# A planner inside the kernel that sets the order in which every engine is queued (hybrid encoder step, one core)

## The chip, the core and the metric

The kernel runs on one core of a Trainium2 chip. Its engines are named as the profile names them: PE is the matrix engine (PEld its weight loads), DVE the vector engine, ACT the scalar engine, POOL the GpSimd engine, SP the engine that issues the DMAs. Each engine works through one queue in order. The metric is the device time of one execution in microseconds (us); lower is better.

## The reference, cut to what matters

One layer of a streaming encoder is computed for 2048 prompt frames and 32 sample frames of width 1024, which share the weights. Every sub-layer is wrapped in an RMSNorm before and one after:

```
h  = rmsnorm(x);  qa,ka,va,qb,kb,vb,g_low,r = split(h @ w_in)
oa = band_attention(qa, ka, va)         # 8 heads x 64, own 64-frame chunk and the 8 before, relative bias
ob = gla_recurrence(qb, kb, vb, gates)  # 4 heads, key 64, value 128
x  = x + rmsnorm(concat(oa, norm(ob) * silu(r)) @ w_o)
mk, mv = rmsnorm(mem) @ w_mk, rmsnorm(mem) @ w_mv
x  = x + rmsnorm(softmax((h @ w_mq) mk^T) mv @ w_mo)           # 4 heads x 256, 256 memory tokens
x  = x + rmsnorm((silu(h @ w_gate) * (h @ w_up)) @ w_down)     # hidden width 2816
```

All arithmetic is in float32; the new keys, values, states and memory keys and values are outputs too.

## The kernel before

The 2080 frames are handled in three stages, which this document calls A, B and C. Between them only DRAM buffers are passed on (names ending in d: x1d, h1d, h2d, x2d), and each stage opens SBUF and PSUM pools of its own.

- Stage A is the parallel mixing: projections (tiles wqa, wka, wva, wvr), band attention (scores s, softmax u, its transposes pt, prt, products po, o), the linear attention (names that begin with g), the memory keys and values (mkps, mkf, mkt; mvps, mvf), and the output projection w_o (wops), whose rows of 512 or 544 frames are normalised and scaled at lines 751 and 759 (tiles y, acc). The projection of the first memory queries (mqps0) is in it too.
- Stage B is the memory attention in five blocks of 416 frames: queries mqps, scores ms, transposes mpt, values mpv, output mops. A block ends in mem_fin: norm n3, residual (L1000, L1001), norm n4, scaling (L1005). Squares are summed by DVE and POOL (L104), and a matmul with ones (n3_4, n4_4 for the last block) spreads the sum.
- Stage C is the SwiGLU in three blocks of two halves, each product of four blocks done as seven: X, Y and Z are its PSUM tiles (pg for gate, pu for up), mf0 to mf6 the seven operands of a block, made by ffn_ops from the rows hr; pdn is the down projection, which DVE adds into acc.

A float32 product is done as three float32r matmuls: split() writes a rounded copy on ACT (L84) and subtracts it from the source on DVE or POOL (L88), for weights (wg_s, wu_s, wd, wmo_s, wo_s from raw tiles ending in _r) and activations (mf, mv, om) alike:

```
def split(hi, lo, src, lo_eng=None):
    ACT.copy(hi, src)
    ...
    lo_eng.tensor_tensor(out=lo, in0=src, in1=hi.bitcast(F32), op=ALU.subtract)
```

The kernel's Python traces the instructions in program order. Work of two kinds is interleaved as it is traced: weave() sorts lists of work items by their relative place, so that attention and projections alternate. The order in which an engine's queue is filled is then set by the framework's scheduler, which follows the data, the buffers and a priority. The priority is the program order, pulled forward by hand in places: high_priority(offset=PRI) with PRI = 4000 for weight loads and their splits, 8000 for the last mem_fin, and led() with offsets of -3000 to 3000 for single operations. The scheduler works over the stage seams: weights of stage C are loaded and split while stage B still runs.

Of the kernel before, what the change touches and what calls it, by code (L numbers as in the profile page):

```python
# [2 lines left out]

# [5 lines left out]
F32 = mybir.dt.float32  # L9
F32R = mybir.dt.float32r  # L10
# [3 lines left out]
PSUM = bass.MemoryType.PSUM  # L14
DRAM = bass.MemoryType.DRAM

P = 128
# [24 lines left out]
    return out  # L42


@with_exitstack
def encoder_step(ctx, tc, ins, outs):
    nc = tc.nc
    PE, ACT, DVE, POOL, SP = nc.tensor, nc.scalar, nc.vector, nc.gpsimd, nc.sync
# [6 lines left out]
    dpool = ctx.enter_context(tc.tile_pool(name="dpool", bufs=1, space=DRAM))  # L55
    RW = dict(reuse_waits="tile")

    PRI = 4000
    QLEAD = 0.5
    ident = cpool.tile([P, P], F32, name="ident")  # L60
    with tc.high_priority(offset=2 * PRI):
        SP.dma_start(ident, ins["c_ident"])
# [33 lines left out]
    def norm_fm(pool, pspool, xs, n, name, tag="dense", rbufs=2):  # L96
        acc = pool.tile([P, n], F32, tag="nacc", name=name + "_acc")
        for k in range(KT):
            if k == 0:
                ACT.activation(acc, xs[k], AF.Square)  # L100
            else:
                sq = pool.tile([P, n], F32, tag="nsq", name=f"{name}_sq{k}")
                ACT.activation(sq, xs[k], AF.Square)
                (POOL if k % 2 else DVE).tensor_tensor(out=acc, in0=acc, in1=sq, op=ALU.add)  # L104
        ps = pspool.tile([P, 512], F32, tag=tag, name=name + "_ps")
        PE.matmul(ps[:, :n], lhsT=ones, rhs=acc, start=True, stop=True)
        return rstd_of(pool, ps[:, :n], n, D, name + "_r", rbufs)
# [8 lines left out]
    def w_piece(wp, src, name, lo_eng=None):  # L116

        kk, m = src.shape[1], src.shape[2]
        with tc.high_priority(offset=PRI):
            raw = wp.tile([P, 544], F32, tag="wraw", name=name + "_r")[:, : kk * m].rearrange("p (k m) -> p k m", k=kk)  # L120
# [24 lines left out]
    def weave(*lists, lead=1.0):  # L145

        todo = [((i + 0.5) / len(items) * (1.0 if li else lead), li, i, it) for li, items in enumerate(lists) for i, it in enumerate(items)]
        return [it for *_, it in sorted(todo, key=lambda x: x[:3])]
# [36 lines left out]
    with ExitStack() as ph:  # L185
# [13 lines left out]
        def xtile(name):  # L199
            return xp.tile([P, 1088], F32, tag="xw", name=name)  # L200


        def norm_tile(src, tn, g, x_dst, h_dst, name, t_in=None, t_out=None, dst=None):

            xt = xtile(name + "_xt")[:, :D] if t_in is None else t_in
            with tc.high_priority(offset=0 if t_in is None else 2 * PRI):
                SP.dma_start(xt[:tn], src)
# [161 lines left out]
        anti = up.tile([P, P], F32, tag="prt", bufs=2, name="anti")  # L369
# [56 lines left out]
        turn = [0]  # L426
# [274 lines left out]
        def merge(*lists, lead=1.0):  # L701
            for it in weave(*lists, lead=lead):
                it()
# [102 lines left out]
        def mem_q0():  # L806
            n = CB[0][1]
            mv = {}

            def first():  # L810
                mv.update(load_mov(h1d[0][:, :n], n, "hq0"))

            def query(m):
                w = load_w(wp, ins["w_mq"][0], m * P, P, f"wmq0_{m}")
                ps = pd.tile([P, 512], F32, tag="dense", name=f"mqps0_{m}")
                mm3(ps[:, :n], [(w[k], (mv[k][:, 0, :n], mv[k][:, 1, :n])) for k in range(KT)])
                qf = sp.tile([P, 544], F32, tag="st", name=f"qf0_{m}")[:, :n]
                ACT.mul(qf, ps[:, :n], 0.0625)
                SP.dma_start(qmd[0][m * P : (m + 1) * P, :], qf)

            return [first] + [partial(query, m) for m in range(KT)]
# [12 lines left out]
        for b in range(NB):  # L834
# [8 lines left out]
            elif b == NB - 2:  # L843
                kv1, kv2 = mem_kv()
                o1, o2, fin = out_proj(0)
                dense = proj(b + 1, mvs[b + 1])
                dense = dense[:-2] + o1 + dense[-2:] + o2 + kv1[:1] + weave(fin, kv1[1:])
            else:
                p1, p2, pfin = out_proj(1)
                o1, o2, fin = out_proj(2)  # L850
                q0 = mem_q0()
                dense = p1 + p2 + kv2[:1] + weave(pfin, kv2[1:]) + o1 + o2 + q0[:1] + weave(fin, q0[1:])
            merge(attn(b), dense, lead=LEAD[b])
        o1, o2, fin = out_proj(NB - 1)
        merge(o1 + o2 + fin)


    lo_set[0] = [POOL, DVE]
    dense_lead[0] = 0
    with ExitStack() as ph:  # L860
# [28 lines left out]
        def mem_h(b):  # L889
            s, n = CB[b]  # L890
            mv = []
            for k in range(KT):
                raw = hp.tile([P, 416], F32, tag="hr", name=f"h1_{b}_{k}")
                for bb, lo, hi, off in pieces(BLK, s, s + n):
                    led(200, SP.dma_start, raw[:, off : off + hi - lo], h1d[bb][k * P : (k + 1) * P, lo:hi])
                m_ = (mpa if k < 5 else mpb).tile([P, 2, 416], F32R, tag="mov", name=f"m2_{b}_{k}")
                split(m_[:, 0], m_[:, 1], raw)
                mv.append(m_)
            return mv
# [77 lines left out]
        def mem_out(b, mo):  # L977
            s, n = CB[b]
            y = []

            def tile_m(m):
                w = load_w(wp, ins["w_mo"][0], m * P, P, f"wmo{b}_{m}")
                ps = pd.tile([P, 512], F32, tag="dense", name=f"mops{b}_{m}")
                mm3(ps[:, :n], [(w[k], (mo[k][:, 0], mo[k][:, 1])) for k in range(KT)])
                yt = xps[b % 2].tile([P, 416], F32, tag="xy", name=f"y2_{b}_{m}")
                led(3000, DVE.tensor_copy, yt, ps[:, :n])
                y.append(yt)

            return [partial(tile_m, m) for m in range(KT)] + [partial(mem_fin, b, y)]

        def mem_fin(b, y):
            s, n = CB[b]
            last = b == len(CB) - 1
            with tc.high_priority(offset=2 * PRI if last else 0):
                r = norm_fm(np_, pn, y, n, f"n3_{b}")
# [14 lines left out]
        out = []  # L1010
        for b in range(len(CB)):
            mo, heads = mem_attn(b)
            fill = [partial(mem_q, b + 1, mv, m) for m in range(KT)] if b + 1 < len(CB) else out
            for it in weave(heads, fill, lead=QLEAD):
                it()
            if b + 2 < len(CB):
                mv = mem_h(b + 2)
            out = mem_out(b, mo)
            if b != len(CB) - 2:
                for it in out:  # L1020
                    it()


    wph.close()
# [3 lines left out]
    with ExitStack() as ph:  # L1028
# [60 lines left out]
        def unit_w(src, g, name):  # L1089

            with tc.high_priority(offset=PRI):
                raw = []
# [52 lines left out]
        for b, (s, n) in enumerate(CF):  # L1145
# [16 lines left out]
            def down_w(f):  # L1162

                row = []
                with tc.high_priority(offset=PRI):
                    raw_d = wp.tile([P, KT, P], F32, tag="wraw", name=f"wd{b}_{f}_r", bufs=WRB)
# [112 lines left out]
            last = b == len(CF) - 1  # L1279
            held = None  # L1280
            for g in range(NF // 2):
# [6 lines left out]
                if g and not (last and g == NF // 2 - 1):  # L1288
                    down([g - 1], [held])
                    held = None  # L1290
                if g < NF // 2 - 1 or not last:
                    held = u
# [4 lines left out]
            else:  # L1297
# [7 lines left out]
                down(gs, us, (0,), dn)  # L1305
                finish_rows(0, xts)


_INS = ["x_prompt", "x_sample", "mem_prompt", "cache_a_k", "cache_a_v", "state_gla", "cache_mem_k", "cache_mem_v",
        "g_pre_mix", "w_in", "w_alpha2", "b_alpha", "g_gla_out", "w_o", "g_post_mix", "g_pre_mem", "g_mem",  # L1310
# [48 lines left out]
```

## Time and profile before

| | |
|---|---|
| median of 3 runs | 3494.17 us (3490.74 to 3494.37) |
| the profiled execution | 3494.23 us, of which the span is 3492.5 us |
| PE busy | 3314.3 us, 95% of the span, 22211 matmul records |
| DVE, ACT, POOL busy | 2346.2, 1677.8, 1328.7 us |
| mean granted clock of PE | 0.975 |
| DMA | 488.56 MB, 140 GB/s |

A matmul of plain float32 has two records, so 22211 records stand for 20341 matmuls. The span runs from the first to the last instruction. An idle time in the profile is put down to the operation that ended it.

### The profile page before, as it was taken

How to read it: one execution, taken by the hardware profiler on the slowest of the kernel's cores; microseconds unless marked ns; L12 is line 12 of the kernel's file. 1: busy time of each engine (PE TensorE's matmuls, PEld its weight loads, DVE VectorE, ACT ScalarE, POOL GpSimd, SP SyncE). 2: the span in 40 equal slices, each digit the busy share in tenths (PEclk: the TensorE clock that was granted, in tenths of full speed). 3: DMA queues.
4: the chain of work that ended last, by engine and by line, in shares of the span. 5: the costliest groups of instructions: out<-in, count | busy, mean ns of one | idle time of the engine just before them, and what ended most of it. 6: DMA issues, size and time to landing. Idle time of an engine off the chain costs nothing. (4 is left out here: it accounts for less than half of the span.)

```text
span 3492.5 us, 60178 instructions
## 1 busy us (share of the span) xinstructions
PE 3314.3 (95%) x22211; PEld 3115.0 (89%) x22211; DVE 2346.2 (67%) x4395; ACT 1677.8 (48%) x3733; POOL 1328.7 (38%) x1086
## 2 busy tenths in 40 slices
PE   8999999999998989899999789999899999999998
PEld 6888888989987778789999689999899999899998
DVE  5578767665558687486666685666976667866665
ACT  5455455554445555465555443333543334533334
POOL 3242132132134433444543453333453334533332
PEclk9999999999999999999999899999999999999999
DMA  9855644555347455664645542222242223222222
GB/s 274 273 179 161 206 147 152 163 172 159 121 134 227 142 182 174 206 213 146 192 150 169 174 133 78 78 73 73 87 144 73 75 78 94 91 92 73 73 73 90
DMA packets 550044, 488.56 MB, mean 140 GB/s; under 512 B 48488, under 2 KB 496801, under 8 KB 549749
## 3 DMA queue, kind: packets, MB, share of 16 engines
q1 hardware_dynamic: 549749, 484.71, 45.0%
q8 instruction: 174, 2.85, 0.3%
q14 instruction: 121, 0.99, 0.1%
HBM read 369.68 MB, written 114.91 MB: 139 GB/s over the span
## 5 line engine op out<-in xcount | busy, mean ns | idle before, releaser
L81 PE MATMUL pdn<-u,wd 128*128 128x346 f32 (+1 forms) x3168 | 528.0, 324 | 11.5 <-DVE up L1049 9.8
L81 PEld LDWEIGHTS pdn<-u,wd 128*128 128x128 f32 x3168 | 511.8, 191 | 14.0 <-DVE up L1049 10.4
L84 ACT CAST wg_s<-wg_r 128x512 fp32r<-128x512 f32 x231 | 139.5, 620 | 409.5 <-PE pdn L81 200.4
L81 PE MATMUL pg_X<-mf,wg_s 128*128 128x346 f32 (+1 forms) x1584 | 283.9, 328 | 8.7 <-DVE mf L88 3.3
L1049 DVE TENSOR_TENSOR acc<-acc,pdn 128x346 f32<-128x346 f32 (+1 forms) x464 | 231.0, 510 | 87.1 <-PE pdn L81 87.0
L81 PE MATMUL pu_X<-mf,wu_s 128*128 128x346 f32 (+1 forms) x1584 | 282.2, 323 | 0.0
L81 PEld LDWEIGHTS pg_X<-mf,wg_s 128*128 128x128 f32 x1584 | 260.8, 193 | 12.6 <-ACT mf L84 4.6
L81 PEld LDWEIGHTS pu_X<-mf,wu_s 128*128 128x128 f32 x1584 | 258.1, 190 | 0.4
L88 POOL TENSOR_TENSOR wu_s<-wu_r,wu_s 128x512 fp32r<-128x512 f32 x132 | 175.8, 1333 | 212.1 <-ACT wu_s L84 202.9
L88 POOL TENSOR_TENSOR wg_s<-wg_r,wg_s 128x512 fp32r<-128x512 f32 x99 | 136.3, 1378 | 299.6 <-ACT wg_s L84 289.0
L81 PE MATMUL wvr_ps<-wvr_s,mv 128*128 128x256 f32 (+3 forms) x1632 | 222.8, 286 | 1.3 <-DVE wvr_s L88 1.3
L81 PE MATMUL wops<-om,wo_s 128*128 128x512 f32 (+1 forms) x960 | 203.8, 363 | 15.4 <-ACT om L84 14.5
L81 PE MATMUL mops<-mo,wmo_s 128*128 128x416 f32 x960 | 201.8, 360 | 12.1 <-DVE wmo_s L88 8.7
L88 POOL TENSOR_TENSOR u<-sg,u 128x346 fp32r<-128x346 f32 (+1 forms) x132 | 134.9, 1033 | 195.9 <-ACT u L84 195.9
L81 PEld LDWEIGHTS wvr_ps<-wvr_s,mv 128*128 128x128 f32 (+1 forms) x1632 | 202.9, 183 | 6.0 <-DVE wvr_s L88 1.8
L81 PEld LDWEIGHTS mops<-mo,wmo_s 128*128 128x128 f32 x960 | 179.7, 192 | 18.2 <-DVE wmo_s L88 9.5
L81 PEld LDWEIGHTS wops<-om,wo_s 128*128 128x128 f32 x960 | 157.0, 194 | 39.9 <-ACT om L84 15.3
L448 PE MATMUL po<-prt,v 128*128 128x128 f32 x1120 | 177.0, 282 | 12.0 <-DVE o L453 6.5
L84 ACT CAST wu_s<-wu_r 128x512 fp32r<-128x512 f32 x231 | 136.4, 618 | 87.5 <-DVE wu_r L1049 34.1
L448 PEld LDWEIGHTS po<-prt,v 128*128 128x128 f32 x1120 | 153.7, 195 | 19.6 <-DVE o L453 7.7
L81 PE MATMUL mqps<-m,wmq_s 128*128 128x416 f32 x768 | 163.0, 361 | 6.1 <-DVE wmq_s L88 6.1
L81 PEld LDWEIGHTS mqps<-m,wmq_s 128*128 128x128 f32 x768 | 143.0, 191 | 9.9 <-DVE wmq_s L88 7.0
(410 smaller groups left out, 7884.3 us busy)
## 6 DMA issues: line engine op xcount, KB each, us to landing
wg_r<-in_w_ffn_gate_dram SPq DMA_DIRECT2D x66, 512.0 KB, 3.8
wu_r<-in_w_ffn_up_dram SPq DMA_DIRECT2D x66, 512.0 KB, 4.2
wd_r<-in_w_ffn_down_dram SPq DMA_DIRECT2D x66, 512.0 KB, 3.5
wmq_r<-in_w_mq_dram SPq DMA_DIRECT2D x80, 256.0 KB, 2.9
wmo_r<-in_w_mo_dram SPq DMA_DIRECT2D x80, 256.0 KB, 2.9
wo_r<-in_w_o_dram SPq DMA_DIRECT2D x64, 256.0 KB, 3.1
ks<-kad SPq DMA_DIRECT2D x28, 512.0 KB, 5.1
wvr_r<-in_w_in_dram SPq DMA_DIRECT2D x48, 256.0 KB, 3.3
```

What stands on the lines that cost most here:

```text
L81: return f(*a, **k)
L84: ACT.copy(hi, src)
L88: lo_eng.tensor_tensor(out=lo, in0=src, in1=hi.bitcast(F32), op=ALU.subtract)
L448: PE.matmul(po[:, e * P : e * P + n], lhsT=v[:kk, j, :], rhs=prt[:kk, j, :n], start=j == 0, stop=j == len(rows) - 1)
L1049: eng.tensor_tensor(out=out, in0=a, in1=b, op=ALU.add)
```

## The change

A class Order is added. At the end of each stage order.queue() is called; it takes the instructions traced since the last call, and adds an edge without a semaphore from each instruction to the next one on the same engine, in the order that it has planned. The instructions, the tiles and the pools stay as they are, and so do weave, the priorities and the leads, which from here on decide only where no edge does (between stages, and among instructions that the planner leaves out, such as table loads).

The plan is made by laying the stage out in time. Each instruction has a duration and a delay until others see its result (_cost). _read works out who waits for whom from the cells of the tiles that are read and written. _pass then runs the stage forward: an engine that is free takes the ready instruction with the best rank, provided that the pool buffers it needs are free; SP's DMAs take 450 ns to issue and land after a bandwidth model. The first ranks are the framework's priorities. Afterwards the stage is run backward, and the distance of each instruction to the end of that run becomes its rank; after three such rounds the shortest plan is kept. Nothing is known of other stages: each plan starts with idle engines and ends with its own last instruction.

```
+class Order:
+    ENGINES = ("PE", "Activation", "DVE", "Pool", "SP")
+    SLOW = 1.1
+    PASSES = 3
...
+    def _cost(self, ins, kind, eng, outs, inps):
+        n = self._free(outs[0])
+        slow = self.SLOW
+        if eng == "PE":
+            if any(a.tensor.name.startswith(("ident", "anti")) for a in inps):
+                return (max(30.0, n * 0.86) if n < 128 else 110.0), 250.0
...
+            t = n * 0.4385 + 6.5
+            return (max(t, 111.0 if n >= 128 else 60.0) if n < 256 else t), 250.0
+        if eng == "SP":
+            return 450.0, 2200.0
...
+        elif eng == "Activation":
+            if kind == "InstActivation":
+                t = 170 + n * 0.9 + (195 if len(outs) > 1 else 0)
+            else:
+                t = 165 + n * (0.87 if outs[0].dtype == F32R else 0.82)
+        elif eng == "Pool":
+            t = 170 + n * 2.35
+        elif kind == "InstTensorCopy":
+            t = 150 + n * 1.05
+        elif kind == "InstTensorTensor":
+            t = 200 + n * 1.15
...
+        elif kind == "InstTensorScalarPtr":
+            t = 120 + n * 0.83 if len(inps) < 3 else (230 + n * 1.75 if n > 256 else 200 + n * 1.4)
...
+        return t * slow, 90.0
...
+    def _pass(self, prio, back=None):
...
+                for e, heap in enumerate(ready):
+                    while idle[e] and heap:
+                        _, i = heappop(heap)
+                        stop = None
+                        for k in self.uses[i]:
+                            g = self.tag[k]
+                            if not held[k] and (free[g] <= 0 or head[g] != place[k] or (back is None and self.first[k] != i)):
+                                stop = g
+                                break
...
+                        start[i] = now
+                        fin = now + dur[i]
...
+                            if e == 4:
+                                moved = max(moved, fin) + self.size[i] / 300.0
+                                seen = max(fin + 1900.0, moved + 1300.0)
...
+    def queue(self):
...
+        for turn in range(self.PASSES + 1):
+            start, end = self._pass(prio)
+            if best is None or max(end) < best[0]:
+                best = (max(end), start)
+            if turn == self.PASSES:
+                break
+            back, fin = self._pass([-(s + d) for s, d in zip(start, self.dur)], back=end)
+            whole = max(fin)
+            prio = [whole - b for b in fin]
+        start = best[1]
+        tail = {}
+        for i in sorted(range(n), key=lambda i: (start[i], i)):
+            e = self.eng[i]
+            if e in tail:
+                self.tc.add_manual_dep(self.ops[i], self.ops[tail[e]].name, self.edge, reason="order of issue")
+            tail[e] = i
...
+    order = Order(tc)
...
+    order.queue()
```

Line numbers in the new kernel are 302 higher from the body of encoder_step on. The pieces below are the order of the built programs, before and after, at three places. A name ends in the number of its tile; "x8" stands for eight equal instructions in a row.

The first place is DVE's queue in stage A, where block 0's output rows y1_0 are scaled (L759, after: L1061) while the keys of the memory are projected; mkf5 is the copy of such a projection out of PSUM, which PE then transposes. Before:

```order
L571 TENSOR_SCALAR g12_la_13144<-g12_z_13142 128x256
L572 SCALAR_TENSOR_TENSOR g12_la_13144<-g12_la_13144,g12_z_13142 128x256
L88 TENSOR_TENSOR om1_7_13176<-om1_r7_13174,om1_7_13176 128x512
L759 SCALAR_TENSOR_TENSOR y1_0_0_11344<-y1_0_0_11344,g_pre_mem_1172,acc1_0_11348 128x512 x2
L759 SCALAR_TENSOR_TENSOR y1_0_1_11345<-y1_0_1_11345,g_pre_mem_1172,acc1_0_11348 128x512 x2
L759 SCALAR_TENSOR_TENSOR y1_0_2_11346<-y1_0_2_11346,g_pre_mem_1172,acc1_0_11348 128x512 x2
L759 SCALAR_TENSOR_TENSOR y1_0_3_11347<-y1_0_3_11347,g_pre_mem_1172,acc1_0_11348 128x512 x2
L575 TENSOR_TENSOR g12_la_13144<-g12_la_13144 128x256
L785 COPY mkf5_13007<-mkps5_12982 128x256
```

The eight scalings stand in one run ahead of mkf5. The same part of DVE's queue after:

```order
L390 TENSOR_TENSOR wmk6_4_s_13031<-wmk6_4_r_13029,wmk6_4_s_13031 128x512
L1061 SCALAR_TENSOR_TENSOR y1_0_0_11344<-y1_0_0_11344,g_pre_mem_1172,acc1_0_11348 128x512
L1087 COPY mkf5_13007<-mkps5_12982 128x256
L1061 SCALAR_TENSOR_TENSOR y1_0_0_11344<-y1_0_0_11344,g_pre_mem_1172,acc1_0_11348 128x512
L1061 SCALAR_TENSOR_TENSOR y1_0_1_11345<-y1_0_1_11345,g_pre_mem_1172,acc1_0_11348 128x512 x2
L1061 SCALAR_TENSOR_TENSOR y1_0_2_11346<-y1_0_2_11346,g_pre_mem_1172,acc1_0_11348 128x512
L877 TENSOR_TENSOR g12_la_13144<-g12_la_13144 128x256
L1087 COPY mkf6_13059<-mkps6_13034 128x256
```

One scaling is left ahead of mkf5; the rest stands behind it and between other work.

The second place is PE's queue at the seam from stage B to stage C. Before:

```order
L81 MATMUL mops4_7_23159<-mo4_3_1_22619,wmo4_7_4_s_23156 128x416 x3
L106 MATMUL n3_4_ps_23209<-n3_4_acc_23186,ones_66 128x416
L81 MATMUL pg0_0_X_23437<-mf0_0_23374,wg0_0_s0_23412 128x348 x12
L81 MATMUL pg0_0_Y_23438<-mf0_1_23378,wg0_0_s1_23417 128x348
L81 MATMUL pg0_0_Z_23439<-mf0_5_23392,wg0_0_s5_23431 128x348
L81 MATMUL pu0_0_X_23566<-mf0_0_23374,wu0_0_s0_23541 128x348 x12
```

In between stand 128 matmuls of stage C before n4_4 comes. After:

```order
L383 MATMUL mops4_7_23159<-mo4_3_1_22619,wmo4_7_4_s_23156 128x416 x3
L408 MATMUL n4_3_ps_22869<-n4_3_acc_22846,ones_66 128x416
L408 MATMUL n3_4_ps_23209<-n3_4_acc_23186,ones_66 128x416
L408 MATMUL n4_4_ps_23277<-n4_4_acc_23254,ones_66 128x416
L383 MATMUL pg0_0_X_23437<-mf0_0_23374,wg0_0_s0_23412 128x348 x12
L383 MATMUL pg0_0_Y_23438<-mf0_1_23378,wg0_0_s1_23417 128x348 x12
```

n4_3 and n4_4 have moved ahead of the first matmul of C. On DVE the scalings of blocks 3 and 4 of stage B stand ahead of most of C's first subtractions now, and on ACT the splits of C's first weights but one stand behind B's last squares.

The third place is DVE's queue at the seam between blocks 0 and 1 of stage C, where the operands mf1 of block 1 are made from hr1 while pu0_10 and pdn0_9 run. Before:

```order
L1046 TENSOR_TENSOR hr1_01_26887<-hr1_11_26890,hr1_01_26887 128x4x346
L88 TENSOR_TENSOR mf1_1_27738<-hr1_00_26884,mf1_1_27738 128x4x346
L88 TENSOR_TENSOR wd0_20_0_27905<-wd0_20_r_27903,wd0_20_0_27905 128x512
L1049 TENSOR_TENSOR up0_10_01_27463<-pu0_10_c2_27629,pu0_10_Y_27625 128x348
L1046 TENSOR_TENSOR hr1_00_26884<-hr1_11_26890,hr1_00_26884 128x4x346
L1049 TENSOR_TENSOR acc0_1_23400<-acc0_1_23400,pdn0_9_0_1_27775 128x348
L1049 TENSOR_TENSOR acc0_1_23400<-acc0_1_23400,pdn0_9_1_1_27783 128x348
```

Large subtractions stand ahead of the first copy to up, and alternate with the additions to acc. After:

```order
L1463 TENSOR_TENSOR sg0_10_10_27462<-sg0_10_10_27462,pu0_10_X_27624 128x348
L1352 TENSOR_TENSOR hr1_01_26887<-hr1_11_26890,hr1_01_26887 128x4x346
L390 TENSOR_TENSOR wd0_21_0_27913<-wd0_21_r_27911,wd0_21_0_27913 128x512
L390 TENSOR_TENSOR mf1_1_27738<-hr1_00_26884,mf1_1_27738 128x4x346
L1352 TENSOR_TENSOR hr1_00_26884<-hr1_11_26890,hr1_00_26884 128x4x346
L390 TENSOR_TENSOR mf1_4_27749<-hr1_01_26887,mf1_4_27749 128x4x346
L390 TENSOR_TENSOR mf1_2_27743<-hr1_00_26884,mf1_2_27743 128x4x346
L1352 TENSOR_TENSOR hr1_10_26893<-hr1_10_26893,hr1_00_26884 128x4x346
L1355 TENSOR_TENSOR acc0_1_23400<-acc0_1_23400,pdn0_9_0_1_27775 128x348
```

The copies to up and the products sg have moved ahead of the large subtractions, and the additions to acc behind them.

More of the change, by code (lines that the diff above doesn't have):

```diff
@@ L2 @@
 from functools import partial
+from heapq import heappop, heappush
 import concourse.bass as bass
@@ L1021, in encoder_step @@
                     it()
+    order.queue()
     wph.close()
@@ L1306, in encoder_step @@
                 finish_rows(0, xts)
+    order.queue()
 _INS = ["x_prompt", "x_sample", "mem_prompt", "cache_a_k", "cache_a_v", "state_gla", "cache_mem_k", "cache_mem_v",
```

220 lines of the change are left out of this document (added).

## The prediction

> **What bounds the kernel now.** The first view is the busy time of each engine by stretch, cut at the stage seams that the timeline shows. Its columns are the stretch, its length, the busy time of each engine with the count of its instructions, the granted TensorE clock, the DMA share and GB/s.
>
> ```profile
> core 0: us, PE busy (x) PEld busy (x) DVE busy (x) ACT busy (x) POOL busy (x), PEclk, DMA share, GB/s
> 0.00:30.00 30.00, 16.70 (x96) 15.05 (x96) 16.33 (x39) 17.87 (x45) 14.48 (x36) 0.83 0.85 220
> 30.00:1480.00 1450.00, 1372.25 (x10455) 1217.52 (x10456) 967.54 (x2216) 753.33 (x1840) 471.49 (x409) 0.97 0.59 180
> 1480.00:1935.00 455.00, 438.40 (x2529) 418.79 (x2527) 309.40 (x535) 255.81 (x605) 198.29 (x142) 0.99 0.55 172
> 1935.00:2040.00 105.00, 73.07 (x332) 64.45 (x333) 84.47 (x87) 46.26 (x81) 57.86 (x38) 0.80 0.58 180
> 2040.00:2450.00 410.00, 408.75 (x2560) 406.88 (x2560) 260.72 (x426) 169.04 (x330) 160.73 (x130) 1.00 0.26 82
> 2450.00:2560.00 110.00, 97.57 (x573) 92.99 (x572) 100.60 (x127) 54.99 (x96) 61.00 (x43) 0.94 0.28 89
> 2560.00:2940.00 380.00, 379.92 (x2396) 379.32 (x2395) 238.10 (x393) 151.73 (x298) 146.27 (x121) 1.00 0.28 89
> 2940.00:3050.00 110.00, 97.29 (x570) 92.01 (x569) 100.54 (x129) 55.04 (x98) 61.50 (x43) 0.94 0.28 87
> 3050.00:3440.00 390.00, 390.00 (x2463) 389.93 (x2464) 237.87 (x398) 154.58 (x304) 149.57 (x124) 1.00 0.28 85
> 3440.00:3492.50 52.50, 40.33 (x251) 38.09 (x250) 30.63 (x53) 19.18 (x42) 7.50 (x7) 0.89 0.23 69
> sum 3492.50, PE 3314.27 PEld 3115.05 DVE 2346.18 ACT 1677.83 POOL 1328.70; mean PE 331.43 PEld 311.50 DVE 234.62 ACT 167.78 POOL 132.87
> ```
>
> PE is the bound everywhere: 3314.3 of 3492.5 us. An order of the same instructions can take two things from it: its idle time, 178.2 us, and the clock. The clock is low only in stretches that hold waits: 1.00 where PE is idle for 1.25 us or less (2040 to 2450, 2560 to 2940, 3050 to 3440), 0.80 where it is idle for 31.9 of 105 us. Stage A (30 to 1480) has 77.8 us of idle time, stage B (1480 to 1935) 16.6, the seam from B to C (1935 to 2040) 31.9, the two seams between blocks of C 12.4 and 12.7, head and tail 13.3 and 12.2. The steady parts of C, 1180 us, have nothing to give.
>
> One wait shows how the clock follows it (the third row is the longest wait of stage A):
>
> ```profile
> 219.51 0.33 PE L81 MATMUL s<-ks,qs 128*128 128x128 f32 x1 [2.18 <-DVE u_mn L81]
> 221.00:228.00 7.00, 7.00 (x25) 5.00 (x26) 6.25 (x8) 2.24 (x6) 3.71 (x3) 0.53 0.55 168
> 1443.01 0.82 PE L81 MATMUL wops<-om,wo_s 128*128 128x272 f32 x2 [10.71 <-ACT om L84]
> ```
>
> After 2.18 us of waiting the clock stands at 0.53 for 7 us, a loss of about 3.3 us. For a stretch the loss is at most its length times one minus the clock; since some of that time is itself idle, I count four fifths: 1450 x 0.03 x 0.8 = 35 us in stage A, 455 x 0.01 x 0.8 = 3.6 us in B. The Trainium skill ("TensorE: Matmul & The Clock Gate", section "HAM oscillation — how this bites in real kernels") sets the limit higher, no idle gaps of more than about 3.4 us; the trace differs with its 2.18 us. By that rule only three waits of stage A (10.7 us, and 4.9 and 4.0 in the list below) would cost clock, the clock term would be near 10 us, and the time below would come out at about 3426 us.
>
> **What PE waits for in stage A.** The waits of PE from 30 to 1430 us: engine, line, the waited-for engine and line, then us, times and the longest.
>
> ```profile
> PE s L81 <- DVE u_mn L81: 7.1, 6, 2.6
> PE po L448 <- DVE o L453: 6.5, 5, 2.6
> PE po L448 <- ACT prt L499: 5.2, 5, 1.7
> PE mkt L789 <- DVE mkf L785: 5.1, 2, 4.9
> PE mvps L81 <- DVE mvf L800: 4.0, 1, 4.0
> PE wops L81 <- ACT om L84: 3.8, 3, 2.5
> PE pt L498 <- ACT prt L499: 3.7, 6, 1.3
> PE g_o L639 <- DVE at L628: 3.4, 5, 1.6
> PE g_s L624 <- DVE g_W L604: 2.9, 1, 2.9
> PE wqa_ps L81 <- ACT mv L84: 2.6, 2, 2.1
> PE ss L81 <- DVE sks L278: 2.4, 1, 2.4
> ```
>
> They add up to 46.7 us, of which DVE's are 31.4 (67%), and with the casts of om and mv on ACT 37.8 (81%). These are short operations that stood late in a queue. The longest shows it:
>
> ```profile
> 1093.00 9.44 DVE L759 SCALAR_TENSOR_TENSOR y<-y,g_pre_mem,acc 128x512 f32<-128x512 f32 x8 [0.17 <-ACT acc L734]
> 1103.16 0.69 PE L789 MATMUL mkt<-ident,mkf 128*128 128x128 f32 x2 [4.93 <-DVE mkf L785]
> ```
>
> Eight scalings that nobody hurries for hold DVE for 9.44 us, and the copy of mkf, for which PE waits 4.93 us, stands behind them. In the new order the copy of mkf5 stands behind one scaling, and the others are spread: the planner ranks by the longest path to the stage's end, and PE's path goes through the copy.
>
> **The change, term by term.** Nothing is added or removed: the same 20341 matmuls, 1882 DMAs and vector work, every queue rewritten, SP's and POOL's too. So each term is a wait that goes, stays or is made.
>
> *Stage A.* At stake are 77.8 + 35 = 112.8 us. Waits of the kind shown should go, 67% to 81% by the list; I take three quarters, 84.6 us. The ends are one third (38 us: the planner's figures miss the chip's, and the waits turn up elsewhere) and all of it (113 us).
>
> *Stage B.* 16.6 + 3.6 = 20.2 us by the same three quarters: 15.2 us, ends 5 and 20.
>
> *The seam from B to C.* Each call plans its own stage, and in the new PE order every matmul of C stands behind n4_4, the last of B; before, 128 of them stood ahead of it. The groups of 1935 to 2040 us give the prices (last column: idle time before, and its releasers):
>
> ```profile
> L81 PE MATMUL mops<-mo,wmo_s 128*128 128x416 f32 x168 | 39.2, 390 | 10.7 <-DVE wmo_s L88 7.8 <-DVE y L81 1.6 <-ACT mo L971 1.2
> L106 PE MATMUL n_ps<-n_acc,ones 128*128 128x416 f32 x4 | 2.6, 746 | 2.8 <-POOL n_acc L104 2.8
> L1000 DVE SCALAR_TENSOR_TENSOR y<-y,g_post_mem,n_r 128x416 f32<-128x416 f32 x15 | 18.2, 1279 | 0.0
> L1001 DVE TENSOR_TENSOR y<-y,xr 128x416 f32<-128x416 f32 x4 | 4.3, 1068 | 0.0
> L104 DVE TENSOR_TENSOR n_acc<-n_acc,n_sq 128x416 f32<-128x416 f32 x9 | 7.0, 780 | 2.8 <-POOL n_acc L104 1.5 <-ACT n_sq L103 1.2
> L1005 DVE SCALAR_TENSOR_TENSOR y<-y,g_pre_ffn,n_r 128x416 f32<-128x416 f32 x8 | 7.6, 1004 | 0.0
> L1046 DVE TENSOR_TENSOR hr<-hr,hr 128x1392 f32<-128x1392 f32 x4 | 11.3, 2821 | 0.0
> L88 DVE TENSOR_TENSOR mf<-hr,mf 128x1392 fp32r<-128x1392 f32 x5 | 9.1, 1814 | 5.0 <-ACT mf L84 5.0
> ```
>
> What goes: the 10.7 us of mops, which waited behind C's weights on DVE. What comes: between n3_4 and n4_4 DVE has eight L1000 (10.2 us), four L1001 (4.3), three L104 (2.3) and eight scalings L1005 of block 3 (8.0, of which about 2.3 lie under ACT's Ln and Exp), 22.5 us, and about 2 us of POOL's last addition and the matmul: 24.5 us in which PE has nothing. Behind it twelve matmuls run (3.6 us at half clock), while DVE owes eight L1005 (8.0), two L1046 (5.6), one L88 (1.8) and a short weight operation (0.7) to the second operand: 12.5 us more. With the 2.8 us before n3 and 5 us of small waits that is 45 against 31.9 us: 13 us lost. With POOL out of the way these DVE operations could take half of their means here (end: 2 us gained); with more contention it is 55 us (23 lost).
>
> *The seams inside C.* PE waits where DVE's preparation of the next block stands ahead of the copies out of PSUM:
>
> ```profile
> 2464.62 7.01 PE L81 MATMUL pdn<-u,wd 128*128 128x348 f32 x24 [4.91 <-DVE up L1049]
> L1046 DVE TENSOR_TENSOR hr<-hr,hr 128x1384 f32<-128x1384 f32 x4 | 8.4, 2109 | 0.0
> L88 DVE TENSOR_TENSOR wd<-wd_r,wd 128x512 fp32r<-128x512 f32 x3 | 8.0, 2654 | 0.0
> L88 DVE TENSOR_TENSOR mf<-hr,mf 128x1384 fp32r<-128x1384 f32 x4 | 7.8, 1961 | 0.0
> ```
>
> In the new order the copies into up come first, and then six large subtractions and one wd stand in a row ahead of the additions to acc: 6 x 2.04 + 2.65 = 14.9 us. PE can fill six PSUM buffers of six matmuls meanwhile, 36 x 0.159 (379.92 us for 2396) = 5.7 us. So it waits about 9 us in place of 4.9; the rest of the seam (7.5 us of 12.4) should about halve, because the long scalings of the first output, which held DVE as 6 and 2, now stand as 3, 1 and 4 with weight operations between them. Gain and loss cancel: 0, ends 18 us gained and 17 lost for both seams.
>
> *Head and tail.* Chains of one thing after another, 13.3 and 12.2 us idle: 0, ends 5 either way.
>
> **The sum** against the profiled execution's 3494.2 us (span 3492.5 and 1.7 around it; the median of the runs is 3494.17): 3494.2 - 84.6 - 15.2 + 13 = 3407 us.
>
> **The rivals.**
> *Nearly every wait goes.* For it: the planner multiplies its durations off PE by 1.1, so it plans a copy rather too late than too early, and PE has work behind it. Nine tenths of A and B (120 us), no loss at B to C, 9 us at C's seams: 3365 us.
> *The waits only move.* For it: DVE is busy for two thirds of stage A, and a queue in a fixed order passes each delay on. A third of A and B (45), 13 lost at the seam and 5 in C: 3467 us.
> *Slower.* The mechanism is DVE's unbroken runs at the three seams, held up by POOL. The planner prices a 512-wide subtraction at (200 + 512 x 1.15) x 1.1 = 868 ns whatever POOL does; the wd row shows 2654. At the far ends the seams cost 23 + 17 us and 5 us of clock. It decides once A and B give less than 38 us; at a quarter of theirs (33) and a few lost at the head it ends at 3508 us. The Trainium skill ("SBUF — State Buffer", section "Who interferes with whom") speaks for it: a VectorE instruction with two SBUF inputs and a GpSimd instruction that reads SBUF share a port pair, and the later one is blocked for the whole instruction. The wd row agrees in kind; by that rule alone the seams cost the 40 us above, and the sum would be about 3434 us.
> *No change that can be measured* (0.2%, 7 us): gains and losses cancel by chance. That the order isn't changed at all is out: hardly a row of PE's queue stands where it stood.
>
> **Chances.** Forecast 0.50 (own range 3385 to 3440, from half to all of A and the ends of the seams), nearly everything 0.20, moved waits 0.17, slower 0.08, no change 0.05. Faster by over 0.2% thus 0.87, same 0.05, slower 0.08. The range 3355 to 3472 takes in the forecast, most of the first rival and most of the second.
>
> **What would show it.** Stage A with some 25 us of PE idle time in place of 78 and a clock of 0.99; no wait of mkt for mkf above 1 us; PE idle for over 20 us between the last mops and the first pg_X, and no mops wait for wmo_s; at the seams of C a wait of pdn for acc of 4 to 14 us; busy sums of ACT and POOL within a few per cent. The prediction is wrong if stage A keeps more than half of its idle time, or if B to C costs under 30 or over 55 us.

## The result, and the profile after

The changed kernel takes 3461.35 us (median of four runs, 3458.72 to 3463.02); the kernel before, run beside it on the same chip, 3493.72 us. The ratio is 0.9908 (95% interval 0.9891 to 0.9925). The kernel is 32 us faster, and the forecast was 87 us.

The head of the page of the changed kernel: PE, DVE and POOL have as many instructions as before, and the busy sums are close to those of before (DVE 2% more).

```profile
span 3456.9 us, 60285 instructions
PE 3282.8 (95%) x22211; PEld 3095.9 (90%) x22211; DVE 2395.7 (69%) x4395; ACT 1692.9 (49%) x3730; POOL 1352.5 (39%) x1086
```

PE's idle time is 3456.9 - 3282.8 = 174.1 us, where it was 178.2: the sum hides a gain and a loss of nearly the same size. To find them, both traces are cut where PE has done the same share of its matmul work (each matmul counted with the time from its start to the next one's where nothing holds PE), so that a row of one kernel is as much work as the row of the other. One cut is the prediction's seam between A and B, 1480 us, which in the changed kernel is 1411 us. The columns are the stretch, its length, PE's busy time, the granted clock, the DMA share and GB/s. Before:

```profile
340.00:1035.00 695.00, 680.66 (x5581) 0.99 0.52 158
1035.00:1480.00 445.00, 390.55 (x2746) 0.95 0.60 185
1480.00:1593.00 113.00, 105.06 (x643) 0.97 0.57 179
1593.00:1912.00 319.00, 310.34 (x1753) 0.99 0.57 174
1912.00:2063.00 151.00, 118.74 (x605) 0.86 0.53 166
2425.00:2560.00 135.00, 122.57 (x730) 0.95 0.27 87
```

The same work after the change:

```profile
334.00:1000.00 666.00, 665.20 (x5597) 1.00 0.56 168
1000.00:1411.00 411.00, 385.46 (x2750) 0.96 0.62 188
1411.00:1546.00 135.00, 109.55 (x609) 0.86 0.65 196
1546.00:1861.00 315.00, 309.84 (x1801) 0.99 0.57 173
1861.00:2016.00 155.00, 112.62 (x586) 0.81 0.51 162
2376.00:2518.50 142.50, 122.30 (x735) 0.93 0.28 84
```

Row by row: the first half of stage A became 29 us shorter, its second half 34, the seam from A to B 22 us longer, the rest of stage B 4 shorter, the seam from B to C 4 longer, the first seam in C 7.5 longer. Of the rows not shown, the second seam in C is 7 us longer, the start of A 6 us shorter, the steady parts of C and the tail together 3. That is the whole 35.6 us between the two spans. Inside stage A the planner did most of what was forecast. At the seams, where a planned stage begins or one of C's blocks gives way to the next, nothing was gained, and some 40 us of the 69 were given back.

The two longest waits of PE at the seam from A to B (1425 to 1480 us):

```profile
PE mpv L383 <- ACT vTp L386: 14.5, 1, 14.5
PE mqps L383 <- DVE m L390: 5.2, 1, 5.2
```

The first is followed back from ACT to SP. The cast of vTp had waited 12.6 us for a DMA, and that DMA was issued behind the last results of stage A (the releaser of a row stands in brackets; SPq is the DMA queue's own engine):

```profile
1473.47 0.62 ACT L386 CAST vTp<-vr 128x512 fp32r<-128x512 f32 x1 [12.61 <-DMA vr<-mvd]
```

```profile
1461.76 5.19 SPq L1062 DMA_DIRECT2D h1d<-y  x8
1468.27 0.32 SPq L383 DMA_DIRECT2D xr<-x1d  x1
...
1469.11 0.51 SPq L1190 DMA_DIRECT2D vr<-mvd  x1
```

SP's order shows why. In the kernel before, vr0, the first load of the memory's values, stood well ahead of these results. In the plan of stage B it stands behind xr0_0, a load for the end of B's block 0. Between the two planned chains the framework decides by priority, and xr0_0, traced late, has a low one: every DMA of A's last block goes first, and all that stands behind xr0_0 in B's chain waits with it.

```
1196 L383 DMA h1_2_0_18510<-h1d1_163 128x192
1197 L423 DMA wmq1_3_4_r_18325<-in_w_mq_dram 128x4x128
1198 L383 DMA h1_2_0_18510<-h1d2_164 128x224
1199 L1052 DMA x0r3_2_17591<-x0d3_73 128x544
1200 L1055 DMA x1d3_161<-y1_3_0_17047 128x544
...
1215 L1062 DMA h1d3_165<-y1_3_3_17050 128x544 x2
1216 L383 DMA xr0_0_18882<-x1d0_158 128x416
1217 L423 DMA wmq1_4_0_r_18358<-in_w_mq_dram 128x4x128
1218 L1190 DMA vr0_17734<-mvd_168 128x2x256
```

At the seam from B to C the forecast wait is there, 27.0 us between n3_4 and n4_4:

```profile
PE n_ps L408 <- POOL n_acc L406: 29.0, 2, 27.0
```

In stage C PE waits for the additions to acc, as forecast, but longer. DVE's queue and PE's at the first seam of C:

```profile
2407.49 3.10 DVE L1463 TENSOR_TENSOR sg<-sg,up 128x348 f32<-128x348 f32 x1
2410.52 0.50 DVE L1355 TENSOR_TENSOR up<-pu_c,pu_Z 128x348 f32<-128x348 f32 x1
2410.94 4.25 DVE L1463 TENSOR_TENSOR sg<-sg,up 128x348 f32<-128x348 f32 x2
...
2415.54 1.59 DVE L1352 TENSOR_TENSOR hr<-hr,hr 128x1384 f32<-128x1384 f32 x1
...
2428.06 1.36 DVE L1355 TENSOR_TENSOR acc<-acc,pdn 128x348 f32<-128x348 f32 x3
```

```profile
2409.77 4.93 PE L383 MATMUL pdn<-u,wd 128*128 128x348 f32 x30
2415.67 1.22 PE L383 MATMUL pdn<-u,wd 128*128 128x348 f32 x6 [0.97 <-DVE sg L1463]
2428.62 3.81 PE L383 MATMUL pdn<-u,wd 128*128 128x348 f32 x12 [11.73 <-DVE acc L1355]
```

The six subtractions and the wd take 12.5 us in a row (2415.54 to 2428.06). PE had filled five of its six PSUM buffers (30 matmuls) before that row began, and stopped 1.2 us into it.

### The profile page after: what moved, and what is told of

The parts are those of the page before. It is cut to its first block, busy times and chain, and to the rows that moved or that the text cites. A ratio compares the mean times of both kernels' runs of the same rounds, so it can differ in the third digit from the quotient of the medians.

```text
span 3456.9 us, 60285 instructions
## 1 busy us (share of the span) xinstructions
PE 3282.8 (95%) x22211; PEld 3095.9 (90%) x22211; DVE 2395.7 (69%) x4395; ACT 1692.9 (49%) x3730; POOL 1352.5 (39%) x1086
## 4 chain that ended last, share of the span: by engine, by line
PE 49%; DVE 4%; issue 2%; ACT 1%; DMA 1%; POOL 1%; SPq 0%; DVEq 0%; POOLq 0%; ACTq 0%
PE pdn L383 14%; PE pg_X L383 7%; PE pu_X L383 7%; PE mops L383 5%; PE pg_Y L383 3%; PE pu_Y L383 3%; PE mqps L383 2%; PE pg_Z L383 2%; PE pu_Z L383 2%; PE mpv L383 1%; PE ms L383 1%; DVE y L1304 1%; DVE hr L1352 0%; DVE acc L1535 0%; DVE mf L390 0%
## 5 line engine op out<-in xcount | busy, mean ns | idle before, releaser
L383 PE MATMUL pdn<-u,wd 128*128 128x346 f32 (+1 forms) x3168 | 521.9, 323 | 27.8 <-DVE acc L1355 25.5
L390 POOL TENSOR_TENSOR wu_s<-wu_r,wu_s 128x512 fp32r<-128x512 f32 x132 | 192.1, 1465 | 250.9 <-ACT wu_s L386 245.1
L383 PE MATMUL mops<-mo,wmo_s 128*128 128x416 f32 x960 | 191.1, 354 | 0.0
L383 PEld LDWEIGHTS mops<-mo,wmo_s 128*128 128x128 f32 x960 | 178.2, 188 | 3.7 <-issue 1.1
L750 PE MATMUL po<-prt,v 128*128 128x128 f32 x1120 | 169.6, 278 | 0.0
L383 PE MATMUL pg_Y<-mf,wg_s 128*128 128x346 f32 (+1 forms) x792 | 142.2, 328 | 14.4 <-ACT mf L386 8.3
```

Source lines behind the costliest of these rows:

```text
L383: return f(*a, **k)
L750: PE.matmul(po[:, e * P : e * P + n], lhsT=v[:kk, j, :], rhs=prt[:kk, j, :n], start=j == 0, stop=j == len(rows) - 1)
```

## The experiments

The theory after the result: inside a stage the plan takes waits away, and at its ends it makes new ones. The reasons it gives are that the edges turn each engine's share of a stage into one unbroken chain, and that the rank by longest path doesn't see PSUM buffers. The rivals: stage A's gain is smaller than forecast for reasons of its own; B and C carry the gain; the planner's prices are off. In the edits `order.last = ...` (short for order.block.bb.instructions[-1]) means that what has been traced so far is passed over by the next plan and stands where the framework puts it. All times are medians of four runs; the kernel before took 3491.6 to 3492.1 us beside them.

**The memory's keys and values left out of the plan (kv_free).**

```
         load_kv()
+        order.last = ...
         mv = mem_h(1)
```

> The loads and splits of the memory keys and values at the head of stage B (kr, vr, kTp, vTp) are left out of the plan and stand where the framework puts them; all else as in the changed kernel (3461.4 us). Theory (edges make one in-order chain of SP, and vr0 stands in it behind xr0_0, a load that nobody needs yet and that the framework passes over for 18 DMAs of stage A's last block): vr0 now stands ahead of those DMAs, the 14.5 us wait of mpv for the cast of vTp goes below 2 us, the half clock around it with it, 3440 to 3450 us. The 5 us waits of mqps and sqb_ps beside it stay. Rival (the seam is bound by the chain of A's last block, PE would only stop at the next operand): the idle time from 1425 to 1480 us stays above 20 us, 3455 to 3465 us.

Measured 3467.5 us (ratio 0.9929, 0.9914 to 0.9944): a miss. The wait of mpv went, and another took its place, 11.0 us of ms for mpr, since ACT stood still for the next load of the same chain:

```profile
1477.23 0.54 ACT L386 CAST q<-qf 128x416 fp32r<-128x416 f32 x1 [12.32 <-DMA qf<-qmd]
```

So vr0 was only the first of a row. The place is right and the theory too narrow: it is the chain that stands behind A's DMAs.

**Stage B's DMAs without edges (b_sp_free).** Run after the next three, to test that.

```
-            if e in tail:
+            if e in tail and e not in self.FREE:
...
+    order.FREE = (4,)
     order.queue()
+    order.FREE = ()
```

> All three stages planned as in the changed kernel (3461.4 us), but in stage B the DMAs on SP get no edges; all other engines do. In the order vr0 and the loads qf0_5 and qf0_6 then stand ahead of the DMAs of stage A's last block. Theory (at the seam A to B it is SP's chain that holds PE: in kv_free vr0 was ahead, but the load of qf stood behind the same DMAs and ACT waited 12.3 us for it): no wait above 6 us between 1425 and 1490 us of the kind mpv for vTp or ms for mpr, and 10 to 20 us gained there, 3441 to 3452 us. Rival (the chains of ACT and VectorE, in which A's last squares and B's first casts stand in a fixed order, hold it as well): the idle time at the seam stays near 25 us, 3455 to 3468 us.

Measured 3454.3 us (0.9895, 0.988 to 0.991), 7 us less than the changed kernel by the medians, though the two intervals overlap. Between 1425 and 1490 us PE's waits are now:

```profile
PE sqb_ps L1034 <- DVE acc L1028: 6.9, 1, 6.9
PE mpt L1264 <- DVE mpr L1261: 5.4, 3, 3.8
PE mqps L384 <- DVE m L391: 5.1, 1, 5.1
```

The long wait for a load is gone and no other of its size came; PE is busy for 37.5 of the 55 us from 1425 to 1480, where it was 29.6. All three waits are for DVE. The work of the seam from A to B takes 126 us here (1415 to 1541), where it took 135 in the changed kernel, and 112.5 with B unplanned altogether (plan_a, below). Of the 22 us that the seam lost, SP's chain is thus worth 9, and the chains of the other engines the other 13.

**The last mem_fin left out of the plan (fin_free).**

```
                 for it in out:
+                    if b == len(CB) - 1 and it is out[-1]:
+                        order.queue()
                     it()
-    order.queue()
+    order.last = ...
```

> The last mem_fin (block 4: norms n3_4, n4_4, residual, scaling) is left out of the plan of stage B and of stage C, all else as in the changed kernel (3461.4 us). In the order some 170 matmuls of C then stand ahead of n4_4. Theory (the 27 us wait of n4_4 comes from the chain that holds all of C's matmuls behind it): the wait of n_ps for POOL's n_acc falls below 5 us, PE's idle time from 1900 to 1990 us from 42 to about 10 to 20 us, 3425 to 3441 us. Rival (C's operands wait for the same DVE work of 22 us, so PE stops at pg in place of n4_4): idle time there 32 us or more as in the kernel before, 3450 to 3465 us.

Measured 3456.5 us (0.9901, 0.9884 to 0.9917); that is 5 us less than the changed kernel, and the two intervals overlap. The rival holds. The 27 us wait fell to 6.7, and the operands of C were late instead, one after the other, this one the longest:

```profile
PE n_ps L408 <- POOL n_acc L406: 6.7, 1, 6.7
PE pg_Y L383 <- DVE mf L390: 5.8, 1, 5.8
```

From 1900 to 1990 us PE was still idle for 90 - 52.5 = 37.5 us, against 42.4, and the work of the whole seam took 154.5 us (1858.5 to 2013) against 155. DVE owes the same work to both, and the order mostly chooses which wait is named.

**PSUM readers ranked earlier in stage C (acc_first).**

```
-            prio = [whole - b for b in fin]
+            prio = [whole - b - (self.EARLY if r else 0.0) for b, r in zip(fin, self.drains)]
...
+    order.EARLY = 15000.0
     order.queue()
```

(drains marks the instructions with an input in PSUM; EARLY is 0 for A and B.)

> In the plan of stage C every instruction that reads PSUM is ranked as if it stood 15 us earlier; A and B as in the changed kernel (3461.4 us). In DVE's order at the seam between blocks the additions of pdn0_9 to acc then stand between the large subtractions in place of behind six of them. Theory (the rank by the longest path to the end is blind to PSUM buffers): the two waits of pdn for acc, 11.7 and 11.9 us, fall below 3 us each, and the clock beside them comes back, 3440 to 3447 us. Rival (the wait comes from what the planner misprices, the 512-wide subtractions of wd at 0.87 us that took 2.65 us beside POOL): the waits stay above 8 us or come back as waits of pg for mf, 3456 to 3466 us.

Measured 3458.7 us (0.9904, 0.9889 to 0.9919). The mechanism is as the theory says, the worth is not. At the first seam the wait for acc fell from 12.8 us to 1.5, and weights came late in its place:

```profile
PE pu_X L386 <- ACT wu_s L389: 3.7, 2, 2.7
...
PE pdn L386 <- DVE acc L1358: 1.5, 2, 0.8
```

PE's idle time there fell from 20.2 to 13.8 us, about what it was before the change (12.4). But PE's busy time for the same matmuls rose from 122.3 to 125.9 us, so that the seam as a whole fell only from 142.5 to 139.5 us; why it rose is not settled.

**Only stage A planned (plan_a).** The second order.queue() becomes order.last = ..., the third goes.

> Only stage A is planned, B and C are queued by the framework as in the kernel before. Theory (the plan of A took the inner waits as forecast and the time was lost at the seams, whose B and C sides are free again here): 30 to 1425 us of the changed kernel is kept (about 67 us gained against before in idle time and clock), no 14.5 us wait of mpv, stages B and C as before: 3425 to 3440 us, faster than all three planned. Rival (A's gain is only pushed on into its tail, whatever B does): 3455 to 3475 us. A second rival: B and C planned were worth 15 us and more in sum, and without them it is slower than the changed kernel, above 3470 us.

Measured 3434.9 us (0.9836, 0.9822 to 0.9851): the theory's figure, and faster than both kernels; its interval lies wholly below the changed kernel's. The same cuts of equal work:

```profile
332.00:998.00 666.00, 665.24 (x5600) 1.00 0.55 168
998.00:1417.50 419.50, 388.66 (x2746) 0.95 0.64 197
1417.50:1530.00 112.50, 103.75 (x639) 0.98 0.58 181
1530.00:1851.00 321.00, 310.26 (x1759) 0.99 0.56 172
1851.00:2002.00 151.00, 115.81 (x602) 0.90 0.54 165
2364.00:2500.50 136.50, 123.52 (x729) 0.94 0.28 86
```

The seam from A to B takes 112.5 us in place of 135, as in the kernel before (113): A's chain does no harm while B is free to fill around it. A's second half takes 8 us more than in the changed kernel. The rows of B and C are those of the kernel before within 2 us.

**Stages A and B planned (plan_ab), and stage C alone (plan_c).** The calls of order.queue() for the other stages are taken out.

> Stages A and B planned, C queued by the framework. Theory (planning a stage costs at each seam where a planned queue meets another planned queue, and in C costs without giving): A's gain stays (58 us), the wait of mpv for vTp is there again (about 15 us lost at the seam A to B against plan_a), B itself gives 3 to 5 us, and C's two seams cost nothing (no wait of pdn for acc): 3444 to 3452 us, between plan_a (3434.9) and all three planned (3461.4). Rival (the loss against plan_a is C's alone): 3430 to 3437 us. Rival (C's chain was no harm, the loss is all at the seam A to B): 3455 to 3463 us.

> Only stage C is planned, A and B are queued by the framework. Theory (C has no waits to take away, and DVE's large subtractions stand ahead of the additions to acc at its two seams): slower than before by 10 to 20 us, 3502 to 3512 us, with two waits of pdn for acc of 11 to 12 us. Rival (C's loss comes only where B's planned queues meet it): 3488 to 3496 us.

plan_ab: 3443.4 us (0.9855, 0.9832 to 0.9879; its runs spread over 14 us, more than any other's). The long wait at the seam from A to B is back, and C's waits are those of the kernel before:

```profile
PE mpv L383 <- ACT vTp L386: 14.4, 1, 14.4
PE pdn L383 <- DVE up L1355: 9.9, 2, 5.0
```

plan_c: 3526.6 us (1.0094, 1.0076 to 1.0113), 35 us slower than before, where 10 to 20 were expected. C's inner seams cost 7 to 8 us each, as in the changed kernel, with the same two waits for acc. The rest, which the expectation did not have, is the seam from B to C: 170.5 us for the work that took 151 before.

```profile
1909.00:2079.50 170.50, 124.52 (x605) 0.81 0.48 148
```

The plan's worth by stage, from the three medians: A -57 us (3434.9 against 3491.6), B on top of it +8.5 (the two intervals overlap), C on top of both +18.

**Stage A and B's blocks 1 to 3 planned (plan_a_b_mid).**

```
         for b in range(len(CB)):
+            if b == 1:
+                order.last = ...
+            if b == len(CB) - 1:
+                order.queue()
             mo, heads = mem_attn(b)
```

> Stage A and the blocks 1 to 3 of stage B are planned; B's head and block 0, its last block, and C are left to the framework. Theory (a planned stretch does no harm if unplanned work lies on both of its sides): no wait of mpv for vTp, and B's inner gain of a few us on top of plan_a (3434.9): 3428 to 3434 us. Rival (any planned stretch pays at its ends what it gains inside): 3436 to 3450 us.

Measured 3444.5 us (0.9862, 0.9842 to 0.9883): the rival. With unplanned work on both sides the planned stretch still pays at its start, between blocks 0 and 1:

```profile
PE n_ps L408 <- POOL n_acc L406: 13.1, 1, 13.1
```

Put side by side, the profiled executions show that a plan costs where it begins and not where it ends, so the theory's "at its ends" is half right. The seam from A to B took 113 us before, 112.5 and 113 with A alone planned up to it (plan_a, plan_a_b_mid), and 134.5 and 135 with B's start planned too (plan_ab, the changed kernel). The seam from B to C took 151 us before, 150 behind a planned B with C free (plan_ab), 155 with both planned, and 170.5 with C planned behind a free B (plan_c). Why the last is the longest is not settled.

**Stage A planned with other prices.** As plan_a, with the factor SLOW, which multiplies the planner's durations off PE, changed from 1.1:

```
-    SLOW = 1.1
+    SLOW = 1.3
```

> As plan_a, with the planner's factor on all durations off PE at 1.3 in place of 1.1. Theory (what stays of A's waits from 950 to 1400 us hangs on buffers and chains that no price moves): within 6 us of plan_a, 3429 to 3441 us, the wait of mvps for mvf (6.4 us) still there. Rival (the planner prices VectorE's and GpSimd's work too low, so short operations come late): 3420 to 3428 us, less than 25 us of PE idle time from 30 to 1425 us in place of 38.4.

> As plan_a (3434.9 us, factor 1.1), with the planner's factor on durations off PE at 1.0. Theory (1.3 lost 40 us since its plan holds what the chip does not, so A's gain hangs on prices near the measured ones): 3430 to 3445 us, if the measured durations lie nearer 1.0 than 1.1 somewhat faster. Rival (the gain is a matter of luck, each factor giving some other order with times spread over 40 us): above 3445 us.

> As plan_a (3434.9 us, factor 1.1), with the factor at 1.2. Theory (the loss grows with the mispricing): between the two known times, 3443 to 3465 us. Rival (luck): outside of that, below 3440 or above 3470 us.

> As plan_a (3434.9 us, factor 1.1 on the planner's durations off PE), factor 1.09. Theory (a greedy plan amplifies small changes of price, and 1.1 is one good draw among orders whose times spread over 30 us): not within 6 us of plan_a; 3442 to 3470 us. Rival (a smooth optimum near 1.1, where the planned times fit the chip's): within 6 us, 3429 to 3441 us.

> As plan_a, factor 1.05. Smooth optimum: halfway between 3434.9 (1.1) and 3468.6 (1.0), 3445 to 3458 us. Draws: any time between 3430 and 3475 us, most likely near the three others (3467 to 3474).

> As plan_a, factor 1.15. Smooth optimum: 3445 to 3458 us, halfway between 3434.9 (1.1) and 3467.5 (1.2). Draws: any time between 3430 and 3475 us, and not the same side of the middle as 1.05 by any rule.

| factor | median us | ratio to before (95%) |
|---|---|---|
| 1.0 | 3468.6 | 0.9943 (0.9922 to 0.9964) |
| 1.05 | 3443.5 | 0.9861 (0.9846 to 0.9875) |
| 1.09 | 3436.4 | 0.9842 (0.9827 to 0.9856) |
| 1.1 | 3434.9 | 0.9836 (0.9822 to 0.9851) |
| 1.15 | 3458.1 | 0.9908 (0.9889 to 0.9926) |
| 1.2 | 3467.5 | 0.9937 (0.9919 to 0.9955) |
| 1.3 | 3474.4 | 0.9948 (0.993 to 0.9965) |

For 1.3 the expectation was that no price moves what stays, and it lost 40 us. After 1.0 and 1.2 luck seemed the better reading; 1.09 refuted it. The times lie on a curve with its lowest part at 1.09 and 1.1, and it is steep. Stage A's gain is thus between 17 and 57 us, by a factor of which the trace of before says nothing. Why factors only 5 to 10% off lose 9 to 34 us is not settled. At 1.0 no wait of stage A is longer than 4.3 us; against plan_a, stage A has 17 us more of idle time there, in many short waits, and 15 us more of PE's busy time for the same matmuls.

**PSUM readers ranked earlier in stage A (plan_a_drain5).** The edit of acc_first with EARLY = 5000.0 for stage A, the only one planned.

> As plan_a, and in stage A's plan every instruction that reads PSUM is ranked as if it stood 5 us earlier. In the order the two copies mvf2 stand together behind one scaling of y in place of behind a row of them. Theory (the rank is blind to PSUM buffers in stage A too): the wait of mvps for mvf (6.4 us) falls below 2 us and the idle time from 1002 to 1381 us from 28.7 to about 20 us: 3422 to 3432 us. Rival (a new order is a new draw): the waits named go, others come, above 3440 us.

Measured 3454.9 us (0.9893, 0.9878 to 0.9909), 20 us slower than plan_a: the rival. The wait of mvps for mvf fell from 6.4 to 2.1 us as meant, and others came, the longest of them:

```profile
PE wops L386 <- DVE y L386: 6.5, 2, 5.9
```

## Why the prediction was wrong

The direction was right and the time lay inside the range. It lay beside the rival "the waits only move" (3467 us) by number alone, since that rival gave 45 us to A and B, and A lost 69. The sum failed in these terms:

- **Stage B with its beginning, the step that failed most: -15.2 us forecast, +18 measured.** The prediction shared out the idle time of the row 1480 to 1935 as if the plan could only take waits away there; it asked what a plan makes at a seam only from B to C. The seam from A to B became 22 us longer, with 14.5 us of mpv for vTp, and plan_a shows that it is B's own plan that costs this. In the stretch 1593 to 1912 there were only 8.7 us of idle time to take (319 - 310.3), and 4 us went.
- **Stage A, -84.6 forecast, -69 measured.** The step that failed is "three quarters of 112.8", one share for the whole row from 30 to 1480 us. Of its 77.8 us of idle time 43.6 went, where 58 were forecast: nearly everything in the first half (14.3 to 0.8 us), about half in the second (54.5 to 25.5). The 10.7 us wait of wops for om went as forecast, but these waits stood in the second half after the change:

```profile
PE mvps L383 <- DVE mvf L1102: 6.6, 2, 6.3
PE mkt L1091 <- DVE mkf L1087: 6.6, 3, 2.6
```

  Why they stayed is not settled; ranking PSUM readers earlier shortened the first and gained nothing (plan_a_drain5). The clock term was real: PE's busy time for the same matmuls fell by 25.5 us, where 26 were forecast. That the size fits is partly luck, since the granted clock of the row rose from 0.974 to 0.9864, which is 19 us (1450 x 0.026 - 1381 x 0.0136).
- **The named wait.** mkt for mkf above 1 us was to vanish; it stayed at 6.6 us in three waits, the longest 2.6. The reading of mkf5 came true: its transposes, which had waited 4.93 us, did not wait at all. The three waits are those for mkf1, mkf2 and mkf6, which did not wait before. One copy was followed, and the others were taken to be no worse.
- **The seam from B to C, +13 forecast, +4 measured.** The mechanism and the wait were right (24.5 us forecast, 27.0 measured; no mops waited for wmo_s; 42.4 us idle where 45 were forecast). But PE's busy time for the same work fell from 118.7 to 112.6 us, which the sum did not have: without the waits of mops the part ahead of the long wait ran at full clock, 338 records in 62.0 us, where 342 had taken 67.1 at 0.91.
- **The seams in C, 0 forecast, +14.5 measured.** Two steps failed. The wait for acc was forecast at 9 us and came at 11.7: PE was to fill six PSUM buffers, 5.7 us, while the large subtractions ran, and five were full before they began, since three multiplications beside POOL's work had already held DVE for 7.3 us. The row itself was a little shorter than the estimate (12.5 for 14.9 us). And the rest of the seam did not halve: 8.5 us beside the long wait, 7.5 before. The 4.2 us wait of pu_Z for wu_s went, but the transposes of the output (yt) came to wait 4.8 us, where they had waited 0.7.
- **Head, tail and the steady parts of C, 0 forecast, -3 measured** (the start of A is counted above).

The terms of B (33 us), A (16) and C (14.5) were too good, that of B to C (9) and the last (3) too bad: 51 us, which is 3407 to 3458, and 3458.6 is the profiled execution's time (3456.9 + 1.7). The two readings that were to show the prediction wrong did not see this. For the same work as before (30 to 1411 us) stage A kept 34.2 of 77.8 us of idle time, less than half, and the seam from B to C had 42.4 us, between 30 and 55; what failed lay between these two stretches. The rival "slower" was priced with the right mechanism at C's seams, 17 us at its far end, too small to decide.

The low clock after waits is worth a look, since the prediction rested 35 us on it. At the seam from B to C the clock stood at about half from 1925 to 1985 us, through the 27 us wait and the whole of the uneven work behind it:

```profile
1925.00:1945.00 20.00, 1.56 (x2) 0.55 0.95 302
1945.00:1960.00 15.00, 3.05 (x5) 0.50 0.58 206
1960.00:1985.00 25.00, 13.18 (x42) 0.50 0.36 117
1985.00:1995.00 10.00, 10.00 (x64) 0.99 0.67 190
```

The 42 matmuls of the third row took 13.2 us; at the 0.159 us of a matmul in C's steady part they would take 6.7. That the clock fell beside a wait of 27 us agrees with the rule of the Trainium skill ("TensorE: Matmul & The Clock Gate", section "HAM oscillation — how this bites in real kernels") that long gaps drop the clock to half. The clock was full again once PE had work without a break (the last row).

## What to carry to other kernels

A planner that lays out one stage at a time should be judged at its seams, and most of all where a planned stage begins: list, for each engine, the first rows of the next stage's chain, and ask whether one that nobody needs yet would hold up one that somebody does (here a residual load ahead of the values). Plan the stage that has waits inside and leave the ones without, here A alone, with 3434.9 us the fastest kernel of this study. Before trusting a planner's gain, vary its prices by 5 and 10%: what stays at every price belongs to the plan (here 17 us), the rest to the prices.

## What the hardware showed

A VectorE (DVE) multiplication of 348 columns with both inputs in SBUF took 3.10 us while POOL worked on a 1384-wide subtraction; the additions between, which read PSUM, took 0.50 us at the same time (the rows of the first seam in C above). In C's steady part the same multiplication has a median of 0.52 us:

```profile
L1463 DVE TENSOR_TENSOR sg<-sg,up x21: 506/520/1223, 2069.1 to 2326.6; 128x348 f32<-128x348 f32 x21
```

```profile
2406.68 6.96 POOL L390 TENSOR_TENSOR mf<-hr,mf 128x1384 fp32r<-128x1384 f32 x2 [2.03 <-ACT mf L386]
```

POOL's first of the two ends near 2410.2, the multiplication at 2410.6. In the trace all six such multiplications of C's two seams end 0.37 to 0.38 us after the POOL operation beside them. That is the lock of the Trainium skill ("SBUF — State Buffer", section "Who interferes with whom"), and a VectorE instruction with one input in PSUM goes free of it, as the page says. By the rows, three such multiplications, held for 5.8 us in all, are enough to account for the 2.7 us by which PE's wait for acc was longer than forecast; no run here takes POOL's work away, so that is worked out and not tested.
